# A hybrid decoder trunk on one core: stick-breaking items of a pair's second head taken from longest to shortest, and one weight sum of each strided pair moved from VectorE to GpSimd

## The chip, the cores and the metric

The kernel runs on 1 core of one Trainium2 chip. The metric is the device time of the core in microseconds (us), the median of several runs. TensorE (PE in the profile) multiplies matrices, VectorE (DVE) and ScalarE (ACT) do elementwise work and may read TensorE's accumulators in PSUM, GpSimd (POOL) does elementwise work on SBUF alone, and SyncE (SP) issues the DMA transfers. Each engine takes its own instructions in order; an instruction that waits for another engine holds everything behind it on its queue.

## What is computed

Two layers of: RMSNorm, two token mixers side by side, a gated merge with an output projection and a residual; then RMSNorm, a gated ConvFFN and a residual. Sequence 1024, width 1024. Mixer A is dilated sliding-window attention with 12 heads in three groups (dilations 1, 4, 16). Mixer B, where the first edit lies, is stick-breaking attention with 4 heads, causal:

```
z = einsum('bhqc,bhkc->bhqk', q_blk, kt) * scale          # 128 queries at a time
log_stay = where(causal, log_sigmoid(-z), 0.0)
later = cumsum(log_stay, axis=3, reverse=True) - log_stay
attn = where(causal, exp(log_sigmoid(z) + later), 0.0)
o = einsum('bhqk,bhkc->bhqc', attn, vt)
```

Query block i sees i+1 key blocks of 128, so late blocks are long and early ones short. The second edit lies in the input projection `proj = h @ w_in[l]`.

## The kernel before, in words

Each layer is a mixer and an FFN. The FFN (some 700 us) is not touched. In the mixer, TensorE's instructions are issued in the order in which the program is written (`manual_schedule(engines={PE})`); the order on DVE, ACT and POOL is set by the framework's scheduler, with some parts marked as urgent.

**The items.** `mixer` builds a list of attention items and hands it to `attend`. First come 16 stick-breaking items, B00 to B07 for the first pair of heads and B10 to B17 for the second: item i of a pair is head i // 4 of the pair and quarter q = i % 4 of the queries (L1187; 256 queries, two rows of blocks). Then come 4 items N of the near window and 16 items T of the two strided groups. One stick-breaking item (`stick_item`, from L602) has two scores and q+1 steps. Score a makes the logits of one row of L = 128 (2q+a+1) keys in PSUM (L584, L585), masks the last block on DVE (L623), takes two sigmoids on ACT into `beta` and `stay` (L624, L625), runs a product scan over `stay` on DVE (L627) and multiplies (L628). Each step then turns blocks of the weights on TensorE (L638, `turn`), splits them into a high and a low part (ACT cast and DVE subtraction, L129 and L130), and multiplies them with the values (L649, `apply`). `ob`, all the items' output, is written to DRAM behind the last item (L660).

`attend` interleaves: while item n takes its steps, the two scores of item n+1 are put between them, in the first 70% of n's steps. After every action the object `dense` advances by 0.68 (0.85 and 0.88 or 0.77 for N and T) *shares*, each a slice of some projection's matmuls (six of 128x512 in most). So TensorE has filler work while a score's chain runs through ACT and DVE. The filler is a queue: keys and queries of the second pair, values and keys and queries of the near window (which wait for the scores of B07 and of B17 to be issued), and 14 small products of the strided pairs, `ahead`.

**The strided pairs.** 14 projections a layer (four key/query pairs, two of values, eight of gates) are done as pairs with a seven-product scheme, `pair_rest`. `load` brings two weight blocks of 512 KB into `in_a`, a tile with two buffers. `run` then makes weight sums: a21 + a22 on POOL (L1011), a21 - a11 on DVE (L1014), split by `piece` into w6 (ACT cast, DVE subtraction), and a12 - a11 and a22 - a11 on POOL (L1017, L1018; the second waits until w6 has been read from a11). Seven products of 12 matmuls each follow (`seven`, L889 to L891), and DVE adds their results (L1031 to L1057). These units are the filler of the T items, whose own chain is: two scores into PSUM (L584, L585), a sum with the position bias and a row minimum on DVE (L797), an exponential on ACT (L798), a turn on TensorE (L805 to L807), the split into p1h (ACT) and p1l (DVE, L130), and the product with the values (L815, L817). The w_lo of L130 in the profile is the low part of a weight piece, whichever it is.

Of the kernel before, what the change touches and what calls it, by code (L numbers as in the profile page):

```python
# [11 lines left out]
ALU = mybir.AluOpType  # L12
# [28 lines left out]
RATE = (0.68, 0.85, 0.88, 0.77)  # L41
# [11 lines left out]
def trunk_kernel(ctx, tc, x, norm1, w_in, b_gate, w_br, w_o, norm2, w_up, conv_w, conv_b, w_down, norm_f, out, depth=None, probe=None):  # L53
    nc = tc.nc
    act, dve, pe, pool = nc.scalar, nc.vector, nc.tensor, nc.gpsimd
# [60 lines left out]
    def bank(tag, name):  # L116
        return ps.tile([P, 512], F32, tag=tag, name=name)

    def small(name, dtype=F32):
        return sb.tile([P, 512], dtype, tag="pt", bufs=PT, name=name)  # L120

    def big(name, dtype=F32):
        return sb.tile([P, 2, T], dtype, tag="e8", bufs=6, name=name)
# [306 lines left out]
    S, B = {}, {}  # L430
# [152 lines left out]
    def scores(o, qt, ql, k):  # L583
        pe.matmul(o, qt, k, start=True, stop=False, skip_group_check=True)  # L584
        pe.matmul(o, ql, k, start=False, stop=True, skip_group_check=True)  # L585

    def parts(src, n, name):

        hi, lo = small(name + "h", F32R), small(name + "l", F32R)
        with tc.high_priority(offset=AHEAD):  # L590
            split(hi[:, :n], lo[:, :n], src[:, :n])
        return hi, lo

    def fold(dst, o):

        n = o.shape[-1]
        tmp = small("fold")
        with tc.high_priority(offset=AHEAD):
            act.copy(tmp[0:64, :n], o[64:128, :])
            dve.tensor_tensor(dst, o[0:64, :], tmp[0:64, :n], ALU.add)  # L600


    def stick_item(pr, s, qp):
        if "ob" not in R:
            R["ob"] = big("ob")
        q, k, vt, ob = R["qb", pr], R["kb", pr], R["vb"], R["ob"]
        hd = 2 * pr + s
        rows, st, shared = {}, {}, {}

        def score(a):  # L610
            i = 2 * qp + a
            L = P * (i + 1)
            bt = rows[a] = sb.tile([P, T], F32, tag="p4", bufs=4, name="beta")
            if a == 0:
                st[0] = big("stay")
            sv = st[0][:, a, :]
            for c0 in range(0, L, 512):
                w = min(512, L - c0)
                z = bank("s", "z")
                scores(z[:, :w], *(t[:, s, i * P : i * P + P] for t in q), k[:, s, c0 : c0 + w])  # L620
                with tc.high_priority(offset=AHEAD):
                    if c0 + w == L:
                        dve.tensor_tensor(z[:, w - P : w], z[:, w - P : w], mask_b, ALU.add)  # L623
                    act.activation(bt[:, c0 : c0 + w], z[:, :w], AF.Sigmoid)  # L624
                    act.activation(sv[:, c0 : c0 + w], z[:, :w], AF.Sigmoid, scale=-1.0)  # L625
            rev = sv[:, 0:L][:, ::-1]
            dve.tensor_tensor_scan(rev, rev, zero[:, 0:1].to_broadcast([P, L]), 1.0, ALU.mult, ALU.add)  # L627
            dve.tensor_tensor(bt[:, 0 : L - 1], bt[:, 0 : L - 1], sv[:, 1:L], ALU.mult)  # L628

        def blocks(kb):  # L630

            return [(j, a) for j in range(2) for a in range(2) if kb + j <= 2 * qp + a]

        def turn(kb):
            tp = bank("t", "sb_t")
            todo = blocks(kb)
            for c, (j, a) in enumerate(todo):
                pe.transpose(tp[:, c * P : c * P + P], rows[a][:, (kb + j) * P : (kb + j + 1) * P], ident)  # L638
            shared[kb] = parts(tp, len(todo) * P, "sb")

        def apply(kb):
            last = kb == 2 * qp
            if kb == 0:
                shared["o"] = bank("o", "sb_o")[:, :256]
            o = shared["o"]
            for j in range(2):
                c = P if last and j else 0
                for p in (0, 1):
                    pe.matmul(  # L649
                        o[:, c:256],  # L650
                        vt[(kb + j) // 4][:, (kb + j) % 4, hd, :],
                        shared[kb][p][:, 256 * j : 256 * j + 256 - c],
                        start=(kb == 0 and j == 0 and p == 0),
                        stop=(last and j == 1 and p == 1),
                        skip_group_check=True,
                    )
            if last:
                fold(ob[64 * s : 64 * s + 64, pr, qp * 256 : (qp + 1) * 256], o)
                if (pr, s, qp) == (1, 1, 3):
                    nc.sync.dma_start(obd, ob)  # L660

        sc = [lambda: score(0), lambda: score(1)]
        return sc, [(lambda kb=kb: turn(kb), lambda kb=kb: apply(kb)) for kb in range(0, 2 * qp + 2, 2)]


# [211 lines left out]
    def half(n, k):  # L877
        return [(H[n][0][:, 4 * k + i, :], H[n][1][:, 4 * k + i, :]) for i in range(4)]

    def piece(src):  # L880
        hi = sb.tile([P, 512], F32R, tag="wh", bufs=4, name="w_hi")
        lo = sb.tile([P, 512], F32R, tag="wl", bufs=4, name="w_lo")
        split(hi, lo, src)
        return hi, lo
# [109 lines left out]
    def pair_rest(dense, l, offs, put, view, grid, kept):  # L994
        raw = []

        def load():
            raw.append(sb.tile([P, 4, 512], F32, tag="ql", bufs=2, name="in_a"))
            for c in range(2):
                nc.sync.dma_start(  # L1000
                    raw[0][:, 2 * c : 2 * c + 2, :].rearrange("p a (k n) -> p (a k) n", n=P),
                    w_in[l][:, offs[c] : offs[c] + P].rearrange("(k p) n -> p k n", p=P),
                )

        def run():
            if not raw:
                assert dense.loads.pop(0) is load
                load()
            a11, a12, a21, a22 = (raw[0][:, i, :] for i in range(4))
            yield  # L1010
            pool.tensor_tensor(a21, a21, a22, ALU.add)  # L1011
            yield
            yield
            dve.tensor_tensor(a11, a21, a11, ALU.subtract)  # L1014
            w6 = piece(a11)
            yield
            pool.tensor_tensor(a12, a12, a11, ALU.subtract)  # L1017
            pool.tensor_tensor(a11, a22, a11, ALU.subtract)  # L1018
            w5 = piece(a21)
            yield  # L1020
            u = sb.tile([P, T], F32, tag="wr", bufs=NRAW, name="u")
            u1, u2 = u[:, HF:T], u[:, 0:HF]
            nc.sync.dma_start(u1, kept)
            yield
            w7 = piece(a11)
            yield
            u5 = small("u5")
            pa, pc = bank("ps", "i_a"), bank("ps", "i_c")
            yield from seven(pa, w6, S[2], True, True)
            r2 = u2  # L1030
            dve.tensor_tensor(view(r2), view(u1), grid(pa), ALU.add)  # L1031
            w3 = piece(a12)
            yield "turn"
            yield
            yield from seven(pc, w5, S[1], True, True)
            dve.tensor_tensor(view(u5), view(u1), grid(pc), ALU.add)
            w4 = piece(a22)
            if dense.loads:
                dense.loads.pop(0)()
            dense.last(0)  # L1040
            yield "turn"
            yield
            yield from seven(pa, w7, S[3], False, True)
            dve.tensor_tensor(view(u5), view(u5), grid(pa), ALU.add)
            put(1, 0, u5, False)
            yield "turn"
            yield
            yield from seven(pc, w3, half(0, 1), False, True)
            dve.tensor_tensor(view(r2), view(r2), grid(pc), ALU.add)
            put(0, 0, r2, False)  # L1050
            dense.last(1)
            yield "turn"
            yield
            for word in seven(pa, w4, S[4], False, True):
                yield "turn"
                yield
            dve.tensor_tensor(view(u1), view(u1), grid(pa), ALU.add)  # L1057
            put(1, 1, u1, False)
            yield

        return run, load

    def pair_kq(dense, l, g, pr):
# [82 lines left out]
    def mixer(l, pending):  # L1146
# [36 lines left out]
        items = []  # L1183
        for pr in range(2):
            for i in range(8):
                needs = ["b1"] if pr else []
                items.append((f"B{pr}{i}", needs, [], RATE[0], lambda pr=pr, i=i: stick_item(pr, i // 4, i % 4)))  # L1187
        for pr in range(2):
            for s in range(2):
                items.append((f"N{pr}{s}", [f"0{pr}"], ["v0"], RATE[1], lambda pr=pr, s=s: near_item(pr, s)))  # L1190
# [684 lines left out]
```

## Time and profile before

| | us |
|---|---|
| median of 3 runs (lowest, highest) | 2755.18 (2748.9, 2756.66) |
| the profiled execution, its own time | 2750.49 |
| its span in the profile | 2748.7 |
| TensorE busy in the span | 2669.9 |
| VectorE busy | 2098.8 |
| GpSimd busy | 699.0 |

The stages can be found on the time axis by the tiles: stick-breaking scans run from 71 to about 228 us in the first layer and from about 1430 to 1592 us in the second; the strided pairs' weight sums run from 269 to 567 us and again until 1931 us. In the waits view a row says who waited for whom, then the total in us, how often, and the longest. A row of the timeline has start, duration, engine, line, operation, tiles, shape and, in brackets, how long the engine was idle before and what ended that.

### The profile page before, as it was taken

Reading aid. Unit: us, or ns where it says so; the run is one execution under the profiler, and the core shown is the slowest. Engines: PE = TensorE matmul, PEld = TensorE weight load, DVE = VectorE, ACT = ScalarE, POOL = GpSimd, SP = SyncE. Lnnn points to the kernel's source line nnn. Section 1 sums busy time; section 2 is a strip of 40 time slices with the busy share of each in tenths; the row PEclk is TensorE's granted clock in tenths of the full one; section 3 lists DMA queues with packets and bytes.
Section 4 is the critical chain, followed back from the end, with each engine's and each line's share of the span. In section 5 each row is a group of like instructions: output and inputs, shape, how many; then the busy total and the mean of one; then the engine's idle time right before and its main releaser. Section 6 shows DMA issues by size and latency. Waiting matters only on the chain. (4 is left out here: it accounts for less than half of the span.)

```text
span 2748.7 us, 36983 instructions
## 1 busy us (share of the span) xinstructions
PE 2669.9 (97%) x13098; PEld 2233.4 (81%) x13098; DVE 2098.8 (76%) x3132; ACT 1330.0 (48%) x2458; POOL 699.0 (25%) x509
## 2 busy tenths in 40 slices
PE   8999999999999999999999999998999999999999
PEld 8877877788888888888888778877888888888888
DVE  5888866676689888897657888665858888988865
ACT  5666533355455545432335665333545455554225
POOL 2004122112224433321220041221222333443110
PEclk9999999999999999999999999999999999999999
DMA  4023488764334444688401234986732434446963
GB/s 151 27 85 112 127 239 218 182 204 150 88 123 151 148 157 139 218 325 318 155 31 38 84 112 145 243 215 174 241 112 79 143 139 165 156 143 244 332 251 123
DMA packets 397637, 445.72 MB, mean 162 GB/s; under 512 B 21660, under 2 KB 318988, under 8 KB 395916
## 3 DMA queue, kind: packets, MB, share of 16 engines
q1 hardware_dynamic: 397452, 443.35, 50.6%
q8 instruction: 104, 1.70, 0.3%
q14 instruction: 81, 0.66, 0.1%
HBM read 300.61 MB, written 142.67 MB: 161 GB/s over the span
## 5 line engine op out<-in xcount | busy, mean ns | idle before, releaser
L130 DVE TENSOR_TENSOR w_lo<-up_a,w_hi 128x512 fp32r<-128x512 f32 x240 | 237.8, 997 | 20.1 <-ACT w_hi L129 20.1
L129 ACT CAST w_hi<-up_a 128x512 fp32r<-128x512 f32 x240 | 149.5, 623 | 183.2 <-PE u_a L890 43.1
L1631 DVE TENSOR_TENSOR x<-x,d_ps 128x512 f32<-128x512 f32 (+1 forms) x228 | 152.4, 673 | 77.2 <-PE d_ps L1625 76.3
L1362 POOL TENSOR_TENSOR cv<-cv 128x512 f32<-128x512 f32 x88 | 132.3, 1515 | 248.7 <-DVE cv L1357 138.9
L130 DVE TENSOR_TENSOR w_lo<-w_raw,w_hi 128x512 fp32r<-128x512 f32 x176 | 131.5, 751 | 65.7 <-ACT w_hi L129 65.2
L129 ACT CAST w_hi<-w_raw 128x512 fp32r<-128x512 f32 x176 | 109.3, 622 | 122.9 <-PE o_ps L156 67.0
L129 ACT CAST w_hi<-in_a 128x512 fp32r<-128x512 f32 x140 | 86.8, 620 | 156.9 <-PE i_a L890 80.9
L130 DVE TENSOR_TENSOR g<-cv,g 128x512 fp32r<-128x512 f32 x154 | 152.6, 992 | 5.3 <-ACT g L129 2.7
L1623 PE MATMUL d_ps<-gd_in,w_hi 128*128 128x512 f32 (+1 forms) x340 | 130.2, 383 | 1.5 <-ACT w_hi L129 1.2
L1625 PE MATMUL d_ps<-gd_in,w_lo 128*128 128x512 f32 (+1 forms) x340 | 129.8, 382 | 0.0
L1624 PE MATMUL d_ps<-gd_in,w_hi 128*128 128x512 f32 (+1 forms) x340 | 129.7, 382 | 0.0
L889 PE MATMUL u_a<-hh,w_hi 128*128 128x512 f32 x320 | 124.7, 390 | 0.3 <-DVE u L1513 0.3
L890 PE MATMUL u_a<-t_lo,w_hi 128*128 128x512 f32 x320 | 124.5, 389 | 0.0
L890 PE MATMUL u_a<-hl,w_hi 128*128 128x512 f32 x320 | 124.5, 389 | 0.0
L891 PE MATMUL u_a<-t_hi,w_lo 128*128 128x512 f32 x320 | 124.5, 389 | 0.0
L889 PE MATMUL u_a<-t_hi,w_hi 128*128 128x512 f32 x320 | 124.5, 389 | 0.0
L891 PE MATMUL u_a<-hh,w_lo 128*128 128x512 f32 x320 | 124.5, 389 | 0.0
L1623 PE MATMUL d_ps<-gd_in,wd 128*128 128x512 f32 (+1 forms) x292 | 113.9, 390 | 0.0
L627 DVE TENSOR_TENSOR_SCAN stay<-stay,zero 128x128 f32<-128x128 f32 (+3 forms) x64 | 89.0, 1390 | 32.6 <-ACT stay L625 32.0
L129 ACT CAST g<-cv 128x512 fp32r<-128x512 f32 x154 | 95.0, 617 | 38.9 <-POOL cv L1362 30.0
L1018 POOL TENSOR_TENSOR in_a<-in_a 128x512 f32<-128x512 f32 x28 | 38.3, 1369 | 294.4 <-DVE w_lo L130 294.4
L1625 PE MATMUL d_ps<-gd_in,wd 128*128 128x512 f32 (+1 forms) x292 | 112.8, 386 | 0.0
(390 smaller groups left out, 8726.6 us busy)
## 6 DMA issues: line engine op xcount, KB each, us to landing
gd<-g SPq DMA_DIRECT2D x154, 512.0 KB, 3.8
gd_in<-gd SPq DMA_DIRECT2D x154, 512.0 KB, 6.2
up_a<-in_w_up_dram SPq DMA_DIRECT2D x80, 512.0 KB, 4.9
in_a<-in_w_in_dram SPq DMA_DIRECT2D x56, 512.0 KB, 6.0
w_raw<-in_w_in_dram SPq DMA_DIRECT2D x104, 256.0 KB, 3.0
t_kq<-tk SPq DMA_DIRECT2D x64, 384.0 KB, 7.4
wd_raw<-in_w_down_dram SPq DMA_DIRECT2D x22, 1024.0 KB, 12.8
gin<-gs SPq DMA_DIRECT2D x32, 512.0 KB, 4.3
```

Source lines behind the costliest of these rows:

```text
L129: act.copy(hi, src)
L130: dve.tensor_tensor(lo, src, f32(hi), ALU.subtract)
L627: dve.tensor_tensor_scan(rev, rev, zero[:, 0:1].to_broadcast([P, L]), 1.0, ALU.mult, ALU.add)
L889: pe.matmul(o, w[0][:, c], rh, start=(first and i == 0), stop=False, skip_group_check=True)
L890: pe.matmul(o, w[0][:, c], rl, start=False, stop=False, skip_group_check=True)
L891: pe.matmul(o, w[1][:, c], rh, start=False, stop=(last and i == 3), skip_group_check=True)
L1018: pool.tensor_tensor(a11, a22, a11, ALU.subtract)
L1362: return lambda: pool.tensor_tensor(dst, a, b, ALU.subtract)
L1623: pe.matmul(o[:, sub], wh[:, c], gh[:, sub], start=(i == 0 and k in (0, 4, 5)), stop=False, skip_group_check=True)
L1624: pe.matmul(o[:, sub], wh[:, c], gl[:, sub], start=False, stop=False, skip_group_check=True)
L1625: pe.matmul(o[:, sub], wl[:, c], gh[:, sub], start=False, stop=(i == m - 1), skip_group_check=True)
L1631: dve.tensor_tensor(x, x, o[:, sub], ALU.add)
```

## The change

The list of items for the second head of each pair runs through the query quarters 3, 2, 1, 0 instead of 0, 1, 2, 3. The pair's order is therefore 0, 1, 2, 3, 3, 2, 1, 0. The condition for writing `ob` is set to the new last item. In `pair_rest`, a21 - a11 is issued on GpSimd's queue, between the two sums that are there already.

```
@@ stick_item, apply @@
-                if (pr, s, qp) == (1, 1, 3):
+                if (pr, s, qp) == (1, 1, 0):
                     nc.sync.dma_start(obd, ob)
@@ pair_rest, run @@
             pool.tensor_tensor(a21, a21, a22, ALU.add)
             yield
             yield
-            dve.tensor_tensor(a11, a21, a11, ALU.subtract)
+            pool.tensor_tensor(a11, a21, a11, ALU.subtract)
             w6 = piece(a11)
             yield
             pool.tensor_tensor(a12, a12, a11, ALU.subtract)
@@ mixer, items @@
-  lambda pr=pr, i=i: stick_item(pr, i // 4, i % 4)))
+  lambda pr=pr, i=i: stick_item(pr, i // 4, 7 - i if i > 3 else i)))
```

More of the change, by code (lines that the diff above doesn't have):

```diff
@@ L658, in apply @@
                 fold(ob[64 * s : 64 * s + 64, pr, qp * 256 : (qp + 1) * 256], o)
-                if (pr, s, qp) == (1, 1, 3):
+                if (pr, s, qp) == (1, 1, 0):
                     nc.sync.dma_start(obd, ob)
@@ L1013, in run @@
             yield
-            dve.tensor_tensor(a11, a21, a11, ALU.subtract)
+            pool.tensor_tensor(a11, a21, a11, ALU.subtract)
             w6 = piece(a11)
@@ L1186, in mixer @@
                 needs = ["b1"] if pr else []
-                items.append((f"B{pr}{i}", needs, [], RATE[0], lambda pr=pr, i=i: stick_item(pr, i // 4, i % 4)))
+                items.append((f"B{pr}{i}", needs, [], RATE[0], lambda pr=pr, i=i: stick_item(pr, i // 4, 7 - i if i > 3 else i)))
         for pr in range(2):
```

## Prediction

> **What bounds the kernel now.** I read the page, then TensorE's waits over the run, then the timeline around each wait.
>
> ```profile
> PE 2669.9 (97%) x13098; PEld 2233.4 (81%) x13098; DVE 2098.8 (76%) x3132; ACT 1330.0 (48%) x2458; POOL 699.0 (25%) x509
> ```
> ```profile
> PE o L815 <- DVE p1l L130: 23.8, 16, 4.4
> PE sb_t L638 <- DVE beta L628: 16.3, 14, 2.2
> PE z L584 <- DVE st L797: 5.0, 2, 2.8
> ...
> PE i_a L889 <- DVE u L1049: 2.3, 2, 1.3
> ```
>
> TensorE is busy 97% of the span, and neither edit takes a matmul away. All that can be won is idle time of TensorE, 2748.7 - 2669.9 = 78.8 us, and what a lowered clock costs after a wait. Two groups of waits lie where the edits are: 16.3 us for the stick-breaking chain, and 23.8 + 5.0 + 2.3 = 31.1 us for DVE work of the T stage.
>
> The first group, at its place (item B17, quarter 3, second layer):
>
> ```profile
> 1585.02 0.40 PE L584 MATMUL z<-kt,qt 128*128 128x512 f32 x1
> ...
> 1591.79 0.27 PE L638 MATMUL sb_t<-ident,beta 128*128 128x128 f32 x1
> ...
> 1592.78 1.22 DVE L628 TENSOR_TENSOR beta<-beta,stay 128x1023 f32<-128x1023 f32 x1
> ...
> 1594.05 0.55 PE L638 MATMUL sb_t<-ident,beta 128*128 128x128 f32 x3 [1.98 <-DVE beta L628]
> ```
>
> The longest row needs 1594.0 - 1585.0 = 9.0 us from score to product, and TensorE's filler before the first turn lasts 1591.8 - 1585.0 = 6.8 us. The long item follows a shorter one, whose steps are too few.
>
> The second group, at its longest:
>
> ```profile
> 504.01 1.26 POOL L1011 TENSOR_TENSOR in_a<-in_a 128x512 f32<-128x512 f32 x1 [3.86 <-DMA in_a<-in_w_in_dram]
> 505.31 0.69 DVE L1014 TENSOR_TENSOR in_a<-in_a 128x512 f32<-128x512 f32 x1 [4.11 <-POOL in_a L1011]
> ...
> 506.08 1.27 POOL L1017 TENSOR_TENSOR in_a<-in_a 128x512 f32<-128x512 f32 x1 [0.80 <-DVE in_a L1014]
> 506.51 1.38 DVE L130 TENSOR_TENSOR w_lo<-in_a,w_hi 128x512 fp32r<-128x512 f32 x1
> 507.81 1.01 DVE L130 TENSOR_TENSOR p1l<-t,p1h 128x384 fp32r<-128x384 f32 x2
> 508.41 0.58 PE L815 MATMUL o<-p1l,t_v 128*128 128x256 f32 x1 [4.40 <-DVE p1l L130]
> ```
>
> Weights land late, POOL's sum starts late, and DVE stands 4.11 us at L1014 with p1l, which TensorE needs, queued behind. This is common:
>
> ```profile
> POOL in_a L1018 <- DVE w_lo L130: 294.4, 28, 35.8
> ...
> POOL in_a L1011 <- DMA in_a<-in_w_in_dram: 104.0, 24, 10.3
> ...
> DVE in_a L1014 <- POOL in_a L1011: 57.5, 21, 4.5
> ```
>
> **The order of the items.** No instruction is added, and the items' steps, hence the filler's shares, are as many as before. Working `attend` through: a quarter 3 behind a quarter 2 has 3 shares between its last score and its first turn; behind a quarter 3 it has 5, as has 2 behind 3, and 1 behind 2 has 3. The ends (0 behind 1, 0 behind 0, 1 behind 0) have 2 shares, which today covers rows of up to 512. Five shares and two more actions make the cover of 6.8 about 11 us, over 9.0. B06, B07, B16 and B17 lose their rising neighbours; B13 keeps its wait, as do the layer's first items.
>
> ```profile
> 140.34 0.55 PE L638 MATMUL sb_t<-ident,beta 128*128 128x128 f32 x3 [1.46 <-DVE beta L628]
> ...
> 215.16 0.55 PE L638 MATMUL sb_t<-ident,beta 128*128 128x128 f32 x3 [0.51 <-DVE beta L628]
> 228.73 0.55 PE L638 MATMUL sb_t<-ident,beta 128*128 128x128 f32 x3 [2.03 <-DVE beta L628]
> ...
> 1503.74 0.55 PE L638 MATMUL sb_t<-ident,beta 128*128 128x128 f32 x3 [1.47 <-DVE beta L628]
> ...
> 1580.49 0.55 PE L638 MATMUL sb_t<-ident,beta 128*128 128x128 f32 x3 [0.53 <-DVE beta L628]
> ```
>
> With 1.98 at 1594.05 these are 1.46 + 0.51 + 2.03 + 1.47 + 0.53 + 1.98 = 8.0 us, all of which I take as gone. The clock follows some waits:
>
> ```profile
> 460.00:470.00 10.00, 6.81 (x22) 5.25 (x21) 4.93 (x7) 1.20 (x2) 2.56 (x2) 0.69 0.41 125
> 500.00:510.00 10.00, 5.60 (x28) 4.64 (x28) 4.58 (x9) 3.19 (x9) 2.68 (x3) 0.91 0.89 217
> 510.00:520.00 10.00, 10.00 (x51) 8.31 (x50) 4.80 (x8) 3.38 (x6) 0.00 (x0) 0.92 0.54 149
> 1500.00:1510.00 10.00, 8.39 (x40) 6.72 (x39) 8.19 (x13) 4.28 (x10) 0.00 (x0) 0.83 0.35 108
> 1790.00:1800.00 10.00, 7.69 (x28) 6.57 (x29) 6.13 (x15) 4.09 (x11) 1.37 (x1) 0.66 1.04 242
> 1870.00:1880.00 10.00, 8.48 (x34) 7.11 (x35) 4.30 (x8) 1.82 (x4) 0.45 (x1) 0.66 0.55 151
> ```
>
> The third column from the right is the granted clock. Around the wait of 1.47 us at 1503.74 it averages 0.83, which is 10 x 0.17 = 1.7 us of lost work; that goes too. The Trainium skill, "TensorE: Matmul & The Clock Gate", section "Why this matters for your kernels", says that throughput drops after gaps of more than about 3 us; by it these 1.7 us would not be there to win, and the total below would be 1.7 us less. The trace does not agree here: the clock fell after 1.47 us, and the row decides.
>
> What may be new is the hand-over to N00. In four steps B17 covered all four of its scores; now two are left uncovered behind a quarter 0. Their cost isn't in the trace. The nearest row is a wait for a score bank there today:
>
> ```profile
> PE z L584 <- DVE st L692: 0.7, 1, 0.7
> ```
>
> Per layer it lies between -0.7 (that wait goes) and +2.8 (the longest wait on L797 above); I take +1, nearest that row. The near window's keys and queries (names 00, 01) end four shares later (56 and 96 instead of 52 and 92), still before they are needed. The write of `ob` stays behind the last item. Sum: -8.0 - 1.7 + 2 = **-7.7 us** (from -11 to -4).
>
> **The sum on GpSimd.** 28 instructions of 0.69 us (505.31 above) leave DVE, and as many come to POOL at the price of their neighbour, 1.29 us.
>
> ```profile
> L1017 POOL TENSOR_TENSOR in_a<-in_a x28: 1267/1294/1684, 279.3 to 1915.5; 128x512 f32<-128x512 f32 x28
> ```
>
> DVE's 28 x 0.69 = 19 us are worth nothing by themselves, since DVE has room; the stall is. POOL's later sums start 1.29 instead of 0.80 us after L1011, so w6, w3 and w7 come 0.49 us later. What hides that: L1018 waits 294.4 us in 28 times for w6's split (above; 10.5 us each), mostly because the slots of the pieces are still in use by matmuls. Without that cover it would be 28 x 0.49 = 14 us. On POOL's queue the moved sum stands between two that wait for the same data, so nothing else gets behind a wait that wasn't behind one before; only the copies of the T items' factors (L855) follow there, and they come twice a layer. What is late next, once the stall goes, is ACT's p1h cast.
>
> Once DVE isn't held at L1014, p1l runs as soon as ACT's cast is done. Not everywhere:
>
> ```profile
> 1789.72 1.64 POOL L1017 TENSOR_TENSOR in_a<-in_a 128x512 f32<-128x512 f32 x1 [0.80 <-DVE in_a L1014]
> 1790.16 1.75 DVE L130 TENSOR_TENSOR w_lo<-in_a,w_hi 128x512 fp32r<-128x512 f32 x1
> ...
> 1792.31 0.47 PE L584 MATMUL z<-t_kq 128*128 128x128 f32 x1 [2.76 <-DVE st L797]
> ```
> ```profile
> 427.21 0.33 PE L584 MATMUL z<-t_kq 128*128 128x128 f32 x1 [2.21 <-DVE st L797]
> ```
> ```profile
> 464.49 0.58 PE L815 MATMUL o<-p1l,t_v 128*128 128x256 f32 x1 [3.19 <-DVE p1l L130]
> ```
> ```profile
> L130 DVE TENSOR_TENSOR w_lo<-in_a,w_hi x65: 673/686/1750, 324.7 to 569.2; 128x512 fp32r<-128x512 f32 x65
> L130 DVE TENSOR_TENSOR p1l<-t,p1h x30: 543/554/559, 409.5 to 567.9; 128x384 fp32r<-128x384 f32 x30
> ```
>
> Here w_lo, with both inputs in SBUF, took 1.75 us instead of 0.69 and ended 0.55 us after POOL's instruction, as if it had started when that ended; p1l, with one input in PSUM, never took over 0.56. Where a w_lo stands ahead of what TensorE needs, POOL's longer run holds it instead of L1014: so at this wait (2.76), at 427.21 (2.21) and at 464.49 (3.19), 8.2 us that I keep. Of 31.1 this leaves 22.9 us to win. The clock adds 0.9 + 0.8 (500 to 520 us) and 3.4 (1870 to 1880 us); the 3.1 and 3.4 us at 460 and 1790 stay with their waits. Against it: 28 longer POOL runs, in which DVE is held 0.5 us longer; of DVE's 57.5 us TensorE saw 31.1, so 28 x 0.5 x 0.54 = 7.6 us at most, nothing at least; I take 3, since p1l is free of it. Sum: -22.9 - 5.1 + 3 = **-25 us** (from -43, all waits and clock, to 0).
>
> Together 2750.5 - 7.7 - 25 = 2717.8. The profiled execution is 4.7 us under the median of the runs; halfway, I forecast **2720**.
>
> **The rivals.**
>
> *The shared port eats it.* The row at 1790.16 is the mechanism: if in most places a w_lo is at DVE's head, the second edit wins nothing and costs up to 7.6 us: 2750.5 - 7.7 + 7.6 = 2750. For it: three of the five waits over 2 us in the T stage have a held w_lo ahead. Against it: p1l is never held. The Trainium skill, "Perfetto Trace Analysis", section "Optimizing Scalar/DVE Operations", states that GpSimd and DVE share a read port, so that offloading between them might not help; the 1.75 us agree.
>
> *The order only moves the waits.* `stay` has one free buffer, so ACT's first sigmoid of the next item waits for the last product of this one; behind a long item now comes another long one. If that gives back the 7.7 us: 2750.5 - 25 = 2725.5.
>
> *The wait goes to ACT, and it is slower.* w6's cast now waits for POOL at ACT's head, with exponentials and p1h behind it. The price: 57.5 + 21 x 0.49 = 67.8 us of waiting, of which TensorE sees a share. It is as much as what goes (31.1 + 7.7 = 38.8) from a share of 57%; at 80% it is 54, hence 2766. Against it: no wait of ACT on L1014 stands in its list; the casts wait for TensorE to free slots.
>
> ```profile
> ACT w_hi L129 <- PE i_a L890: 80.9, 48, 4.5
> ```
>
> *The load becomes the bound.* If TensorE's gain makes L1011's 104 us longer by as much, half of the 25 us stays: 2730.
>
> **How the numbers follow.** The forecast 0.60 (2703 to 2738), the order 0.13, the load 0.05, the port 0.12 (2744 to 2758), ACT 0.10. About 0.3% (8 us) can be told from no change. The first three are faster, and a fourth of the port's: 0.81. The port's middle half and a little of ACT's: 0.09. The rest, slower: 0.10. The range 2703 to 2752 leaves out ACT, the port's upper end and the tail below.
>
> **What would show it.** Right: no wait of DVE on L1011; L815's waits under 8 us; L638's near 8; POOL's L1011, L1014, L1017 back to back. Wrong: ACT waiting for L1014; w_lo's runs for in_a well over their median of 686 ns more often; new waits at the turns of B04 or N00. The scheduler may also order DVE and ACT anew far from the edits, which would make the forecast wrong with both mechanisms right.

## The result, and the profile after

| | before | after |
|---|---|---|
| median of the runs (lowest, highest), us | 2755.92 (2748.9, 2760.78) | 2723.3 (2721.68, 2725.71) |
| ratio to before, 95% interval | | 0.9884 (0.9861 to 0.9907) |
| span of the profiled execution, us | 2748.7 | 2723.9 |

The change saves 1.2%, and the forecast was 2720. The total hides two misses of opposite sign, as the waits of TensorE in the changed kernel show (who waited, for whom, us in total, times, longest):

```profile
PE sb_t L638 <- DVE beta L628: 11.3, 12, 1.9
PE z L584 <- DVE st L692: 8.8, 2, 4.4
PE r_ps L155 <- DVE ql L538: 5.8, 2, 2.9
PE z L584 <- DVE vv L1095: 4.9, 2, 2.5
...
PE z L584 <- DVE st L797: 2.9, 2, 1.5
...
PE o L815 <- DVE p1l L130: 1.5, 2, 0.9
```

The 23.8 us on p1l in the T stage are 1.5, better than forecast (the prediction kept 3.19 us of them). L638 fell from 16.3 to 11.3 instead of 8.3, and three rows are new or much larger (L692, L538, L1095; in the kernel before L692 had 1.4 us and the others none): 19.5 us.

A table by part says where this lies. The borders are four rows of TensorE's timeline: the first turn of a stick-breaking item, the last stick-breaking product, the first score of the T items, and their last product. In the kernel before, first layer:

```profile
72.84 0.71 PE L638 MATMUL sb_t<-ident,beta 128*128 128x128 f32 x3
...
248.71 0.27 PE L649 MATMUL sb_o<-sbl,vb 128*128 128x128 f32 x1
...
401.86 0.22 PE L584 MATMUL z<-t_kq 128*128 128x128 f32 x1
...
577.28 0.27 PE L817 MATMUL o<-p1l,t_v 128*128 128x128 f32 x1
```

In the changed kernel:

```profile
73.45 0.72 PE L638 MATMUL sb_t<-ident,beta 128*128 128x128 f32 x3
...
259.53 0.27 PE L649 MATMUL sb_o<-sbl,vb 128*128 128x128 f32 x1
...
408.60 0.22 PE L584 MATMUL z<-t_kq 128*128 128x128 f32 x1
...
566.43 0.28 PE L817 MATMUL o<-p1l,t_v 128*128 128x128 f32 x1
```

The stick-breaking part went from 248.71 - 72.84 = 175.9 us to 186.1, the part between (near window, then units of filler alone) from 153.2 to 149.1, the T part from 175.4 to 157.8. I call these SB, MID and T below. Filler moves between SB and MID when the order changes, so their sum is what counts. All kernels, first layer / second layer, in us:

| kernel | SB | MID | T | median, us | ratio to before (95%) |
|---|---|---|---|---|---|
| before | 175.9 / 182.1 | 153.2 / 153.2 | 175.4 / 175.6 | 2755 to 2759 | |
| after (both edits) | 186.1 / 190.9 | 149.1 / 149.0 | 157.8 / 156.4 | 2723.3 | 0.9884 (0.9861 to 0.9907) |
| e1_order | 187.6 / 189.3 | 155.3 / 150.8 | 176.3 / 179.7 | 2771.5 | 1.0054 (1.0037 to 1.0072) |
| e2_sum | 177.3 / 182.5 | 153.2 / 153.1 | 158.0 / 159.5 | 2717.7 | 0.9852 (0.9838 to 0.9866) |
| e3_work | 177.2 / 182.2 | 158.0 / 158.1 | 159.8 / 156.6 | 2727.1 | 0.9887 (0.9873 to 0.9902) |
| e4_later | 174.7 / 178.0 | 156.1 / 155.4 | 156.9 / 156.5 | 2716.4 | 0.9853 (0.9836 to 0.9870) |
| e5_work2 | 177.3 / 182.0 | 153.1 / 153.1 | 157.8 / 156.2 | 2717.1 | 0.9847 (0.9832 to 0.9862) |
| e6_pair0 | 177.8 / 181.6 | 154.0 / 153.2 | 157.4 / 158.4 | 2718.6 | 0.9854 (0.9837 to 0.9870) |
| e7_pair1 | 185.0 / 187.3 | 149.1 / 149.0 | 156.5 / 158.8 | 2721.3 | 0.9863 (0.9848 to 0.9879) |
| e8_lean | 176.8 / 177.9 | 149.1 / 149.0 | 156.6 / 156.5 | 2699.3 | 0.9786 (0.9771 to 0.9801) |
| e9_late1 | 187.5 / 189.3 | 149.1 / 149.0 | 156.7 / 157.1 | 2725.6 | 0.9881 (0.9861 to 0.9901) |
| e10_pair1late | 184.9 / 187.8 | 149.1 / 149.1 | 156.8 / 156.5 | 2719.7 | 0.9863 (0.9847 to 0.9879) |
| e11_pair1seven | 171.2 / 176.6 | 155.9 / 156.2 | 157.5 / 157.8 | 2710.7 | 0.9820 (0.9804 to 0.9836) |
| e12_sumlean | 175.7 / 176.2 | 151.7 / 151.9 | 156.6 / 158.7 | 2706.1 | 0.9810 (0.9795 to 0.9824) |

So the changed kernel loses 6.1 and 4.6 us in SB and MID together and wins 17.6 and 19.2 us in T.

**T.** GpSimd's three sums now run back to back, and p1l runs beside them instead of behind a waiting VectorE. The timeline of the changed kernel, GpSimd and VectorE:

```profile
478.48 1.29 POOL L1011 TENSOR_TENSOR in_a<-in_a 128x512 f32<-128x512 f32 x1 [1.92 <-DMA in_a<-in_w_in_dram]
...
479.84 1.71 POOL L1014 TENSOR_TENSOR in_a<-in_a 128x512 f32<-128x512 f32 x1
...
480.32 0.54 DVE L130 TENSOR_TENSOR p1l<-t,p1h 128x384 fp32r<-128x384 f32 x1
...
481.63 1.29 POOL L1017 TENSOR_TENSOR in_a<-in_a 128x512 f32<-128x512 f32 x1
```

**SB.** The loss stands at the hand-over to the near window. Timeline of the changed kernel, with GpSimd's sums of blocks of the activations (`block_sums`, L912 to L914, used by the strided pairs):

```profile
231.60 0.28 PE L649 MATMUL sb_o<-sbh,vb 128*128 128x256 f32 x1
...
232.35 2.70 POOL L912 TENSOR_TENSOR h_sum<-hl 128x512 f32<-128x512 f32 x2 [85.42 <-PE sb_o L649]
...
243.46 2.51 POOL L912 TENSOR_TENSOR h_sum<-hl,hl 128x512 f32<-128x512 f32 x2
...
244.72 7.95 DVE L130 TENSOR_TENSOR w_lo<-w_raw,w_hi 128x512 fp32r<-128x512 f32 x1
245.94 2.51 POOL L913 TENSOR_TENSOR h_sum<-h_sum,hh 128x512 f32<-128x512 f32 x2
...
253.41 0.39 PE L584 MATMUL z<-kt,qt 128*128 128x256 f32 x1 [4.39 <-DVE st L692]
```

One subtraction of VectorE with both inputs in SBUF took 7.95 us, while GpSimd ran sum after sum. The near window's first score operations stood behind it, and TensorE stood 4.39 us. In the kernel before these sums began only at 242.90, when SB was nearly over:

```profile
242.09 0.28 PE L649 MATMUL sb_o<-sbh,vb 128*128 128x256 f32 x1
...
242.90 2.54 POOL L912 TENSOR_TENSOR h_sum<-hl 128x512 f32<-128x512 f32 x2 [20.59 <-PE sb_o L649]
```

`h_sum` takes a buffer of the tag that held the mixer's values. In the new order the last item that reads the values' second half is B15 (its last step's products begin at 231.60), two items before the end of SB. My reading is that this buffer now goes to `h_sum`, while in the kernel before it got that of the first half, last read by B17's second step (242.09). The releases fit it, though no run changes the buffer alone.

**L538.** The second new wait. VectorE in the changed kernel, behind two quarters 3 in a row:

```profile
193.58 2.29 DVE L627 TENSOR_TENSOR_SCAN stay<-stay,zero 128x1024 f32<-128x1024 f32 x1 [1.15 <-ACT stay L625]
195.90 1.23 DVE L628 TENSOR_TENSOR beta<-beta,stay 128x1023 f32<-128x1023 f32 x1
197.05 0.68 DVE L537 SCALAR_TENSOR_TENSOR ql<-q_ps,qt 64x512 fp32r<-64x512 f32 x1
...
198.33 0.69 DVE L538 SCALAR_TENSOR_TENSOR ql<-q_ps,qt 64x512 fp32r<-64x512 f32 x1
```
```profile
199.17 0.47 PE L155 MATMUL r_ps<-hh,w_hi 128*128 128x512 f32 x1 [2.90 <-DVE ql L538]
```

The emptying of the near window's query bank stands behind a scan and a product of the longest row, and the filler stops for 2.90 us.

### The profile page after: what moved, and what is told of

Its sections match the earlier page's. It is cut to its first block, busy times and chain, and to the rows that moved or that the text cites. A ratio compares the mean times of both kernels' runs of the same rounds, so it can differ in the third digit from the quotient of the medians.

```text
span 2723.9 us, 36972 instructions
## 1 busy us (share of the span) xinstructions
PE 2660.4 (98%) x13098; PEld 2233.0 (82%) x13098; DVE 2116.6 (78%) x3104; ACT 1330.3 (49%) x2458; POOL 743.0 (27%) x537
## 5 line engine op out<-in xcount | busy, mean ns | idle before, releaser
L130 DVE TENSOR_TENSOR w_lo<-w_raw,w_hi 128x512 fp32r<-128x512 f32 x176 | 144.4, 823 | 63.0 <-ACT w_hi L129 61.7
L130 DVE TENSOR_TENSOR w_lo<-in_a,w_hi 128x512 fp32r<-128x512 f32 x140 | 114.6, 819 | 3.4 <-ACT w_hi L129 3.2
## 6 DMA issues: line engine op xcount, KB each, us to landing
wd_raw<-in_w_down_dram SPq DMA_DIRECT2D x22, 1024.0 KB, 12.4
```

What stands on the lines that cost most here:

```text
L130: dve.tensor_tensor(lo, src, f32(hi), ALU.subtract)
```

## The experiments

The theory after the result: the moved sum is worth more than forecast, because VectorE's wait was the whole cost; the new order loses time at the hand-over, through GpSimd's earlier block sums. Rivals: the edits do what was forecast, VectorE's work was the cost, or the near window's uncovered scores lose the time by themselves. A "-" line of the diffs is the changed kernel's unless it says otherwise; long lines are shown in part, and the line that makes the tile `spare` is left out.

**e1_order: the order alone.**

```
-            pool.tensor_tensor(a11, a21, a11, ALU.subtract)
+            dve.tensor_tensor(a11, a21, a11, ALU.subtract)
```


> The new order of the items alone; a21 - a11 stays on VectorE. Theory (the order costs time and the sum wins more than forecast): the T stage keeps VectorE's wait at L1014 and p1l's 23.8 us of TensorE wait, and the hand-over from stick-breaking to the near window loses about 6 us a layer, so 2762 to 2770 us, slower than before by 0.2 to 0.5%. First rival (both edits do what was forecast): 7.7 us faster, about 2748. Second rival (the hand-over suffers only together with the moved sum): 2755, no change.

Measured: 2771.5 us, 0.54% slower (0.37 to 0.72%). The direction is the theory's, the size is a little over it. The same place as above, VectorE and TensorE of this kernel:

```profile
239.73 9.07 DVE L130 TENSOR_TENSOR t_lo<-h_sum,t_hi 128x512 fp32r<-128x512 f32 x2
```
```profile
249.19 0.58 PE L584 MATMUL z<-kt,qt 128*128 128x256 f32 x1 [8.27 <-DVE vv L1095]
```

Here the splits of the sums themselves are held (8.47 us in one of the two), and TensorE stands 8.27 us. So the order edit costs time without the other edit too.

**e2_sum: the moved sum alone.**

```
-  stick_item(pr, i // 4, 7 - i if i > 3 else i)
+  stick_item(pr, i // 4, i % 4)
-                if (pr, s, qp) == (1, 1, 0):
+                if (pr, s, qp) == (1, 1, 3):
```


> The moved sum alone; the items stay in the old order. Theory: the whole gain of the T stage without the loss at the hand-over, 2711 to 2718 us, faster than both edits together. First rival (both as forecast): 2731. Second rival (the T stage gained because the new order gives it another start): 2740 or more, and L815's waits on p1l come back.

Measured: 2717.7 us, within the theory's range. Waits of TensorE in this kernel:

```profile
PE sb_t L638 <- DVE beta L628: 16.5, 14, 2.2
...
PE z L584 <- DVE st L797: 3.2, 2, 1.7
...
PE o L815 <- DVE p1l L130: 1.5, 3, 0.7
```

T is 158.0 and 159.5 us. The new order is not needed for that gain, and against this kernel it costs 9.0 us in SB and MID (4.7 + 4.3). By the ratios it is 0.3%, with intervals that touch (0.9861 to 0.9907 against 0.9838 to 0.9866).

**e3_work: VectorE's work put back, without the wait (against e2_sum).**

```
+            dve.tensor_tensor(spare, f32(H[0][0][:, 0, :]), f32(H[0][1][:, 0, :]), ALU.subtract)
```


> The moved sum alone, and VectorE gets an operation of the same 128x512 size with both inputs in SBUF in its place, which reads data that has long been there and whose result nothing uses: the work is back on VectorE, the wait for GpSimd at its head is not. Theory (the wait was the cost): within 6 us of the moved sum alone, 2711 to 2724 us. Rival (the work was the cost): the 28 x 0.69 = 19 us of VectorE and p1l's lateness come back, 2740 us or more.

Measured: 2727.1 us, outside both ranges, and no test of the question. The operations waited for nothing, so the scheduler ran 13 of the first layer's 14 in one bunch ahead of T (336.91 to 358.77 us; the other at 26.43), two at a time at the densest, as VectorE's timeline shows:

```profile
339.91 2.39 DVE L1016 TENSOR_TENSOR spare<-hh,hl 128x512 bf16<-128x512 f32 x2
...
344.99 2.63 DVE L1016 TENSOR_TENSOR spare<-hh,hl 128x512 bf16<-128x512 f32 x2
```

MID grew by 4.8 and 5.0 us, T didn't go back. A probe needs a dependency that keeps it at its place.

**e5_work2: the same work, once in each unit (against e2_sum).**

```
             w6 = piece(a11)
+            dve.tensor_tensor(spare, f32(w6[0]), f32(w6[1]), ALU.subtract)
```


> As in the run before with VectorE's work put back, but the extra operation now reads the two parts of w6, so that it stands once in each unit, behind w6's split: the moved sum alone, 28 more VectorE operations of 128x512 with both inputs in SBUF, no wait for GpSimd's sum at VectorE's head. Theory (the wait was the cost): the T stages keep their 158 and 159.5 us, total 2717 to 2722 us. Rival (the work was the cost): the T stages go back by half or more, towards 175 us each, total 2732 us or more.

Measured: 2717.1 us against 2717.7 without it. The group in this kernel (busy us, mean ns) and TensorE's wait:

```profile
L1017 DVE TENSOR_TENSOR spare<-w_hi,w_lo 128x512 bf16<-128x512 f32 x28 | 27.2, 971 | 0.3
```
```profile
PE o L816 <- DVE p1l L131: 1.6, 4, 0.7
```

27.2 us of VectorE work, more than the 28 x 0.69 = 19.3 that the edit takes away, cost nothing, with T at 157.8 and 156.2 us. The wait was the cost; the rival falls.

**e4_later: both edits, block sums planned later.**

```
-        plan({"B14"}, {0: [third(0)], 6: [third(1)]})
+        plan({"B17"}, {0: [third(0)], 6: [third(1)]})
```


> Both edits, and the first two of GpSimd's block sums (L912 to L914) are released by the last stick-breaking item, with the other two, instead of by the item three before it; no work is left out. Theory (GpSimd's sums hold VectorE's w_lo, 7.95 us at 244.72, and so the near window's first scores): the wait on L692 of 4.4 us in each layer goes, 2714 to 2719 us. Rival (the two scores of N00 are simply left uncovered behind a short item): the wait stays, 2723 us. Third case: the sums, now later, hold the strided pairs' start; T begins later by several us, 2728 or more.

Measured: 2716.4 us, in the theory's range. The waits on L692 and L1095 are gone, as the theory wants. But not in the way that I wrote: the two sums that the edit names run at 42 us in every kernel, since their buffer is free by then. The edit puts the plan's other sums seven steps later, and `h_sum` now starts behind the last stick-breaking item (its last product stands at 247.43 in this kernel). GpSimd, VectorE, ScalarE and TensorE of this kernel:

```profile
247.88 2.54 POOL L912 TENSOR_TENSOR h_sum<-hl 128x512 f32<-128x512 f32 x2 [13.06 <-PE sb_o L649]
```
```profile
243.33 0.69 DVE L130 TENSOR_TENSOR w_lo<-w_raw,w_hi 128x512 fp32r<-128x512 f32 x1
```
```profile
276.57 0.62 ACT L129 CAST t_hi<-h_sum 128x512 fp32r<-128x512 f32 x1 [3.51 <-POOL h_sum L914]
```
```profile
284.37 0.80 PE L155 MATMUL r_ps<-hh,w_hi 128*128 128x512 f32 x1 [3.73 <-ACT q1s L983]
```

w_lo is back at 0.69 us and SB at 174.7, but the sums now collide with the near window's end: ScalarE stands 3.51 us for a sum, with the copy that TensorE needs (L983) later on its queue, TensorE waits 3.73 us for that copy in each layer (1.0 in the kernel before), and MID is 156.1. The collision moved and became cheaper.

**e8_lean: both edits, two of three operations of each block sum left out.**

```
             pool.tensor_tensor(r, f32(al), f32(bl), ALU.subtract)
-            pool.tensor_tensor(r, r, f32(ah), ALU.add)
-            pool.tensor_tensor(r, r, f32(bh), ALU.subtract)
```


> Both edits, with two of the three GpSimd operations of each block sum left out (L913 and L914; the sum is then only the difference of the two low parts). Place, release and order of what is left stay, and VectorE's splits of the sums too. Theory (GpSimd's back-to-back run holds VectorE's operations with two inputs in SBUF): no w_lo over 3 us at the hand-over, L692's waits of 4.4 us fall under 1.5 us, 2708 to 2717 us. Rival (the loss at the hand-over comes from the uncovered scores behind a short item, or from VectorE's own splits put there): L692's waits stay at 3 us or more, 2720 us or more.

Measured: 2699.3 us, below the theory's range of 2708 to 2717. The sums start at the same place, and VectorE's splits there aren't held. GpSimd and VectorE of this kernel:

```profile
232.54 2.67 POOL L912 TENSOR_TENSOR h_sum<-hl 128x512 f32<-128x512 f32 x2 [85.11 <-ACT sbh L129]
```
```profile
243.76 0.68 DVE L130 TENSOR_TENSOR w_lo<-w_raw,w_hi 128x512 fp32r<-128x512 f32 x1
...
245.04 0.69 DVE L130 TENSOR_TENSOR t_lo<-h_sum,t_hi 128x512 fp32r<-128x512 f32 x1
```

SB falls by 9.3 and 13.0 us. VectorE's splits and the uncovered scores are where they were, so these are not the cause; GpSimd's run is. This kernel and the next leave out part of the computation, so their times aren't those of a full kernel.

**e12_sumlean: the same operations left out, in the old order.**

> The moved sum alone, in the old order of the items, with the same two GpSimd operations of each block sum left out (L913 and L914) as in the run with both edits (2699 us). The two runs show what the order is worth when the block sums hold nothing. Theory (the order trades L638's waits for those on L538 and at the values, and its loss was the collision): within 4 us of 2699. Rival (the order gains its 7.7 us once nothing collides): 2704 to 2710 us. Third case (the order costs by itself): 2695 us or less.

Measured: 2706.1 us, the rival's range. With the block sums short, the new order *gains* 6.8 us by the medians (2706.1 to 2699.3; the runs don't overlap, 2704.62 to 2707.55 against 2698.98 to 2702.45, though the ratios' intervals do) and 3.8 us by the spans (2704.4 to 2700.6). With the full sums it costs 5.6 us by the medians (2717.7 to 2723.3). By the spans it costs 2723.9 - 2717.3 = 6.6 us. So the collision is worth 6.8 + 5.6 = 12.4 us by the medians and 3.8 + 6.6 = 10.4 by the spans, both layers together. In SB and MID of the table the gain is only 2.7 us; the rest stands in T, where nothing here ties it to the order. The block sums cost time in the old order as well: without the two operations it is 11.6 us faster (2717.7 to 2706.1). TensorE's waits, this kernel and then e8_lean:

```profile
PE sb_t L638 <- DVE beta L628: 14.4, 12, 2.2
PE o L713 <- DVE p0l L130: 5.8, 6, 2.0
```
```profile
PE sb_t L638 <- DVE beta L628: 10.4, 12, 1.8
PE r_ps L155 <- DVE ql L538: 5.8, 2, 2.9
...
PE o L713 <- DVE p0l L130: 1.9, 4, 0.7
```

The order takes 4.0 us from L638 and 3.9 from the near window's L713, and adds 5.8 on L538.

**e6_pair0 and e7_pair1: the new order in one pair of heads, with the moved sum.**

```
+  stick_item(pr, i // 4, 7 - i if i > 3 and not pr else i % 4)     # e6_pair0
+  stick_item(pr, i // 4, 7 - i if i > 3 and pr else i % 4)         # e7_pair1
```


> The moved sum, and the new order in the first pair of heads only. Theory (the loss sits in the second pair: the hand-over to the near window, and its two longest items in a row beside the projection of the near window's queries): the first pair trades 1.9 us of waits (B06, B07) for about as much behind B11, B12 and the values, so 2715 to 2721 us, as the moved sum alone (2717.7). Rival (the loss is general): about 2721, half of the loss of 6 us a run that both pairs show.

> The moved sum, and the new order in the second pair of heads only. Theory (the loss sits here): block sums start some 10 us earlier and run beside the near window's first scores, L692's wait of 4 us and the wait on L538 of 2.9 us in each layer show, 2723 to 2730 us. Rival (the loss needs both pairs, or comes from the first): 2718 us or less.

Measured: 2718.6 and 2721.3 us; e2_sum has 2717.7. The first is in the theory's range; the second lies between the theory's 2723 to 2730 and the rival's 2718, a miss. The first pair's order changes nothing that can be told. The second pair's lengthens SB to 185.0 and 187.3 us, but MID is 4 us shorter, and the total is not clearly apart (ratio 0.9848 to 0.9879 against 0.9838 to 0.9866). Two rows of e7_pair1:

```profile
237.20 9.08 DVE L130 TENSOR_TENSOR t_lo<-h_sum,t_hi 128x512 fp32r<-128x512 f32 x2
```
```profile
PE z L584 <- DVE vv L1095: 12.0, 2, 9.5
```

The hand-over's waits are the second pair's. That the wait on L538 would show there was wrong: it is 5.8 us with both pairs' order, 0.9 with the first pair's and none with the second's. Why it needs both isn't shown; that the filler is shifted under the two long items is my reading.

**e9_late1 and e10_pair1late: the sums released later, but in one step.** (e10 has the order of e7_pair1.)

```
-        plan({"B14"}, {0: [third(0)], 6: [third(1)]})
+        plan({"B17"}, {0: [third(0), third(1)]})
```


> Both edits, and the first two block sums released by the last stick-breaking item as before, but both in one step, so that the rest of the block sums is not pushed seven steps later. Theory (the block sums cost what they hold up on VectorE, wherever they run): the stick-breaking part keeps 175 and 178 us, the part up to the first strided score goes back from 156 to about 153 us, and the wait of 3.7 us on L983 goes; 2706 to 2713 us. Rival (the sums cost the same wherever they are put; only their place moves): 2716 us, as with the seven steps.

> As the run beside it, with the new order in the second pair only (the first pair rises twice, as in the kernel before). Theory: without the first pair's edit the wait on L538 (2.9 us in each layer) stays away, as it did with the second pair alone; stick-breaking part 172 to 175 us in the first layer, total 2702 to 2710 us, the fastest full kernel. Rival (the block sums' collision costs the same elsewhere): 2714 us or more.

Measured: 2725.6 and 2719.7 us, both misses: no better than after and e7_pair1. GpSimd of e9_late1:

```profile
231.82 2.67 POOL L912 TENSOR_TENSOR h_sum<-hl 128x512 f32<-128x512 f32 x2 [84.71 <-PE sb_o L649]
```

The start is where it was. It isn't the name of the releasing item that counts, it is the seven steps, which, as I read it, put `h_sum`'s first use behind other uses of the tag.

**e11_pair1seven: the moved sum, the second pair's order, and the plan of e4_later.**

> The moved sum, the new order in the second pair only, and the block sums' plan seven steps later (the plan of the run whose block sums began behind the last stick-breaking item). Theory: the block sums begin behind the last item, so the waits on L1095 and L692 at the hand-over stay away; the wait on L538 too, as in both runs with the second pair alone; stick-breaking parts of 172 to 177 us, the part behind them 155 to 156 us, total 2708 to 2714 us. Rival (what the hand-over loses comes back behind it in full): 2716 to 2720 us.

Measured: 2710.7 us, ratio 0.9820 (0.9804 to 0.9836), as the theory said, and the fastest kernel with the whole computation: the hand-over's waits and L538's stay away, though L983's of e4_later stay (7.5 us). Against e4_later, which has the new order in both pairs, it is 5.7 us faster: the first pair's order, which costs nothing that can be told alone (e6_pair0), costs about that beside the second's, 4.4 us of it as waits on L538. No run has the seven steps in the old order, so how much of the 7 us against e2_sum is the order's stays open. GpSimd here:

```profile
245.00 2.55 POOL L912 TENSOR_TENSOR h_sum<-hl 128x512 f32<-128x512 f32 x2 [13.06 <-PE sb_o L649]
```

## Why the prediction was right, and where it was wrong

**What bounds the kernel: right.** Idle time of TensorE at these two places was what could be won.

**The total: luck.** By the medians the change saved 32.6 us (2755.92 to 2723.3) and 32.7 were forecast, but no part came out so. By the spans the sum brought 6.4 us more than forecast, the order 14.3 us less, and the whole 24.8 us; that the median of before lies above its profiled execution made up the rest.

**The sum on GpSimd (-25 forecast): right in mechanism, undersized.** e2_sum shows it alone: -33.5 us in T (17.4 + 16.1), -31.4 us by the spans, 40.8 us by the ratio of its set of runs. The medians show more than the spans because the profiled execution of before lies at the low end of its runs, which spread from 2748.9 to 2769.9 us; what makes them spread stays open. By terms, with e2_sum's rows:
- "8.2 us that I keep", waits with a w_lo held beside GpSimd at VectorE's head: mis-sized. 3.2 + 1.5 = 4.7 us of waits for VectorE stay in all of T, and they went down by 31.1 - 4.7 = 26.4 instead of 22.9 us.
- The clock, 5.1 us: (1 - clock) x 10 us, summed over the 10 us slices from 265 to 580 and from 1620 to 1935 us, went from 11.9 to 3.4 us, so 8.5. With the waits that is 34.9 us, near the 33.5 of T.
- The port, +3: nothing of it shows in TensorE's waits. GpSimd's longer run did slow VectorE (w_lo of in_a went from a mean of 770 to 831 ns, 140 x 0.061 = 8.5 us), and VectorE's spare time took it.
- "VectorE's 19 us are worth nothing by themselves": shown by e5_work2.

**The order of the items (-7.7 forecast): wrong in sign.** Beside the moved sum it costs 9.0 us in SB and MID. The six waits of 8.0 us that it took as gone are gone, so its cover of the long items was right. The step that failed is the hand-over to N00, "+1, nearest that row", bounded by 2.8 a layer. It measured 4.4 + 2.5 us of waits in each layer, with the clock at 0.83 in both slices there (240 to 260 and 1590 to 1610 us). The step asked what the near window's scores would lack in cover; it didn't ask which buffer the new order frees earlier, and what starts then. Two smaller steps failed too: L638's waits went to 11.3 instead of 8.3, mainly since B11 and B12 now wait 0.46 and 1.31 us in the first layer (161.71 and 171.96 us), where before only B12 waited, 0.37 us; and VectorE's load behind two quarters 3 was not looked at (L538, 5.8 us). The term itself was not absurd: with nothing to collide with (e12_sumlean to e8_lean), the order gains 3.8 us by the spans and 6.8 by the medians, 2.7 of it in SB and MID.

**The rivals.** *The shared port*: GpSimd does hold VectorE, but not where I put the cost: in T it shows in no wait of TensorE, at the hand-over it costs 10 to 12 us. The sentence of the Trainium skill quoted with it ("Perfetto Trace Analysis", section "Optimizing Scalar/DVE Operations": offloading between the two engines might not help) would have been a poor guide to the moved sum, which helped by 40 us. *The wait goes to ACT*: ACT's list has no wait on L1014. *The load becomes the bound*: in e2_sum L1011 waits 110.3 us for its load, 104.0 before; no. (In the changed kernel it is 146.3, of which 17.7 and 17.9 us stand before the first pair of each layer, ahead of T.) *The order only moves the waits*: it did worse, but not through `stay`, for which TensorE waits 1.7 us instead of 2.6.

**What would show it.** No wait of VectorE on L1011, L815 under 8 us, the sums back to back: all three as forecast. L638 near 8: no. Of the warning signs two came: the new waits at N00, and w_lo's runs for in_a over 0.9 us, 31 of 140 instead of 20, which in T cost nothing that shows.

## What to carry to other kernels

An operation moved off an engine can be worth the wait that it made at that queue's head; here its own duration was worth nothing. Before the order of work is changed, list which buffers come free earlier and what an idle engine will start in them: a transfer or a GpSimd run that was out of the way may now run beside the place that has the least cover. And an edit that loses can hold a gain: here the second pair's order with the sums seven steps later brings 7 us more than the moved sum alone (2710.7 against 2717.7), though no run tells the order's part from that of the steps.

## What the runs showed of the hardware

- One VectorE operation with two SBUF inputs, usually 0.68 us, took 7.95 us beside six GpSimd operations in a row, and a pair of them 9.07 us, though beside the same sums others took 1.75 us (254.28 in e2_sum). GpSimd's own operations took some 1.25 us each meanwhile (2.51 for two). The 7.95 us ended at 252.67, behind the end of a GpSimd operation at 252.11, and the 1.75 us at 256.03, behind one at 255.48: both some 0.55 us later. What decides whether VectorE gets in behind the first operation or the sixth is open.
- The clock's drops don't follow the length of a wait alone. In the kernel before, waits of 2.17 us at 184.76 and 2.03 us at 228.73 left it at 1.00; in the changed kernel 1.46 us at 431.36 brought 0.83. So neither my reading (a wait of 1.47 us costs 1.7 us more) nor the 3 us of the Trainium skill ("TensorE: Matmul & The Clock Gate", section "Why this matters for your kernels") foretells these drops. The slices, with the clock in the third column from the right, of before:

```profile
180.00:190.00 10.00, 7.83 (x44) 6.58 (x43) 8.67 (x14) 7.24 (x17) 0.00 (x0) 1.00 0.28 84
190.00:200.00 10.00, 10.00 (x56) 8.54 (x55) 6.78 (x12) 5.04 (x11) 0.00 (x0) 1.00 0.53 154
```

and of the changed kernel:

```profile
430.00:440.00 10.00, 8.64 (x40) 7.36 (x41) 6.47 (x16) 4.21 (x11) 3.29 (x3) 0.83 1.09 264
```
